# A hybrid attention and linear-attention layer on one core: the opening with tokens, parameters and modulation blocks laid out by the host

## The chip, the core and the metric

The kernel runs on one core of one Trainium2 chip. The core has five engines that run side by side, each with its own queue of instructions: TensorE (matrix products), VectorE, ScalarE, GpSimd and SyncE. In the profile they are PE (with PEld for its weight loads), DVE, ACT, POOL and SP. Data come from the chip's memory through 16 DMA engines; SP issues nearly all of the transfers, from a queue that keeps its order. The metric is the device time of one execution in microseconds (us). Lower is better.

## The reference: what is computed

One layer over 256 latent tokens `x` and 256 context tokens `ctx`, each of 2048 channels, all in float32. The parts that matter here are the modulated norm at its start and the input projection that follows:

```python
mod_x = split(silu(c)     @ w_mod + b_mod, 6)     # shift, scale, gate, shift, scale, gate
mod_c = split(silu(c_ctx) @ w_mod + b_mod, 6)
h_x = rms_norm(x,   g_mix) * (1 + mod_x[1]) + mod_x[0]
h_c = rms_norm(ctx, g_mix) * (1 + mod_c[1]) + mod_c[0]
proj = h @ w_in          # columns for attention, linear attention, merge gates
```

`rms_norm` divides each token by the root of the mean of its 2048 squares. After the projection come windowed attention with the context as further keys, gated linear attention that starts from the context's end states, a gated merge, an output projection, and a convolutional feed-forward block with its own modulated norm. The output is the latent stream, 256 x 2048.

## The kernel before, in words

**Products.** The 2048 input channels are 16 tiles of 128 partitions (`KT`). Every product in float32 precision is made of three faster ones: an operand is split into a high and a low part, and high x high, high x low and low x high are summed. Weights come in tiles of 128 x 2 x 512 values (`wload`, line 209; 512 KB), and `wsplit_raw` (line 223) makes the high part on ScalarE (line 227) and the low part on VectorE (line 228). `proj_T` (line 277) gives the result with channels on the partitions, in steps of 256 columns; `proj_nat` (line 238) gives it with tokens on the partitions, in steps of 512 columns.

**Modulation.** `mod_both` (line 329) computes shift or scale of `x` and `ctx` for some channel tiles. It loads blocks of `w_mod` of 1 MB each (`mraw`, line 340) and multiplies them with SiLU(c), held in `cS`, by small products that use a quarter of the array each (line 344). The result goes through a transpose on VectorE (line 347), a selecting product `pcol` (line 354), four copies and the addition of the bias (lines 357 and 360).

**The opening (lines 114 to 160 and 549 to 619).** The tokens arrive with tokens on the partitions. The sum of squares of a token block is one instruction, on ScalarE for one block and on VectorE for the other (lines 456 and 457). 32 transposes for `x` and 32 for `ctx` on TensorE (line 465) bring the channels onto the partitions, and copies (lines 471 and 473) take them out of PSUM into `xr`. `factors` makes the norm's factors per token, and `factor_row` (line 483) spreads them as a row by a product of ones with a diagonal matrix. Parameters come as rows through GpSimd's queue and are turned by TensorE (`columns`, line 138). `idle` (line 543) gives TensorE transposes without use, `warm` in the profile.

**Groups.** The input channels are taken in five groups, of 2, 2, 4, 4 and 4 tiles (`groups`, line 433). For each group the modulated, split tokens (`h00hi`, `h00lo` for x, `h10hi`, `h10lo` for ctx) are made by `affine_scale` and `affine_shift`, and then go through four blocks of 512 columns of `w_in`: two with x alone (QB), one with x and ctx (KB, `kbt`), one with x and ctx (VB, `vb0`). The modulation of the next group is computed meanwhile: `bg_steps` holds its steps, and `tick` (line 192) puts some of them between the products, `bg_rate` steps for each weight tile. `mid` is a function called in the middle of a weight tile's products. What has to wait for a result on another engine is put off by `defer`.

**What sets the order.** `load` (line 102) chains the loads of the opening in the order of the program on SP's queue; each waits there until its buffer is free. `pe_seq` (line 74) pins TensorE's instructions to the program's order while `opening` holds something; this ends with the second group. `in_order` fixes the order of single pairs. Buffers of 8 KB per partition come from one pool of 16 (`M`): the tokens, the partial results `kbt` and `vb0` and the split tokens keep some, and the `mraw` blocks use what is left. Weight tiles (`raw`) have seven buffers, their split parts three pairs.

After the groups follow the gates' low-rank product (`wlr`, `plr`, line 679) and the rest of the layer. `mod_latent` (line 365) computes the other modulation parts on VectorE beside later products, with SiLU(c) as a row `csrow`, loaded (line 379) from a copy `csd` in the chip's memory, which line 132 writes. That load's place on SP's queue is left to the planner that orders the instructions.

Of the kernel before, what the change touches and what calls it, by code (L numbers as in the profile page):

```python
# [16 lines left out]
P = 128  # L17
# [9 lines left out]
DFF = 5632  # L27
SCALE = HD ** -0.5


def layer_kernel(ctx, tc, A, out):
# [15 lines left out]
    w_mod = A["w_mod"][0]  # L47
# [49 lines left out]
    def turn_b(*a):  # L97
        return pe_seq(after(PE.transpose(*a)))  # L98

    chain = [None]  # L100

    def load(dst, src):

        d = nc.sync.dma_start(dst, src).ins
        if chain and chain[-1] is None:
# [8 lines left out]
    ident = cst.tile([P, P], F32, name="ident")  # L114
    load(ident, A["k_ident"])
    x00 = M("x00", [P, D])
    load(x00, A["x"][0][0:P, :])
    crow = sm.tile([32, P], F32, name="crow", tag="t128", bufs=2)
    nc.scalar.dma_start(crow[0:16, :], A["c"][0].rearrange("(k p) -> k p", p=P))
    nc.scalar.dma_start(crow[16:32, :], A["c_ctx"].rearrange("(k p) -> k p", p=P))  # L120
    sel = cst.tile([P, 34], F32, name="sel")
    G.dma_start(sel, A["k_sel"])
    ones = cst.tile([P, P], F32, name="ones")
    V.memset(ones, 1.0)

    silu_c = S.activation(crow, crow, AF.Silu)
    with tc.issue_after(silu_c.ins):
        S.preload_act_table_set("natural_log_exp_and_others")
    cS = W2("fb", "cS", [P, KT, 32])
    V.memset(cS, 0.0)  # L130
    csd = dram.tile([KT, P], F32, name="csd")
    G.dma_start(csd, crow[0:16, :])
    pt = bank("pc0", (P, 32))
    PE.transpose(pt, crow, ident[:32, :32])
    for i in range(2):
        V.tensor_copy(cS[:, :, i], pt[:, 16 * i:16 * i + 16])

    def columns(name, parts, eng=G, put=None):
        rows = sm.tile([P, P], F32, name="rows", tag="t128", bufs=2)
        n = 0  # L140
        for ap in parts:
            k = ap.shape[0] // P
            eng.dma_start(rows[n:n + k, :], ap.rearrange("(k p) -> k p", p=P))
            n += k
        t = cst.tile([P, n], F32, name=name)

        def turn():
            pt = bank("pt_" + name, (P, P))
            turn_b(pt[:, :n], rows[:n, :], ident[:n, :n])
            V.tensor_copy(t, pt[:, :n])  # L150

        if put is None:
            turn()
        else:
            put(turn)
        return t

    turn_c1 = []
    c1 = columns("c1", [A["b_mod"][0], A["g_mix"][0], A["g_ffn"][0]], put=turn_c1.append)
    bmod, gmix, gffn = c1[:, 0:96], c1[:, 96:112], c1[:, 112:128]  # L160

# [167 lines left out]
    def mod_both(part, t0, n, dst, put=None):  # L329


        a = []
        c0, w = part * D + t0 * P, n * P
        nk = 16 // n

        def step(k0):
# [3 lines left out]
            load(raw, w_mod[k0 * P:(k0 + nk) * P, c0:c0 + w].rearrange("(c p) d -> p c d", p=P))  # L340
# [24 lines left out]
    def mod_latent(parts, begin=None):  # L365
# [67 lines left out]
    groups = [(0, 2), (2, 2), (4, 4), (8, 4), (12, 4)]  # L433
# [3 lines left out]
    xr = [M(f"xr{i}", [P, 8, T]) for i in range(4)]  # L437
# [4 lines left out]
    def load_tokens(s):  # L442
        x = []
        for t in range(2):
            x_ = x00
            if s or t:
                x_ = M(f"x{s}{t}", [P, D])
                load(x_, A["ctx" if s else "x"][0][t * P:(t + 1) * P, :])
            x.append(x_)
        return x  # L450

    def square(eng, x_, t, ss):

        junk = (kbt, vb0)[t].rearrange("p a b -> p (a b)")
        if eng is S:
            return S.activation(junk, x_, AF.Square, accum_out=ss[:, t:t + 1]).ins
        return V.scalar_tensor_tensor(junk, x_, 1.0, x_, op0=ALU.mult, op1=ALU.mult,
                                      accum_out=ss[:, t:t + 1]).ins

    def turn_tokens(s, t, x_):  # L460
        for g in range(4):
            pt = bank("ptx", (P, 4, P), side=True)
            for k in range(4):
                kt = g * 4 + k
                i = PE.transpose(pt[:, k, :], x_[:, kt * P:(kt + 1) * P], ident)
                if not s + t + kt:
                    opening[:] = [i.ins]
                pe_seq(i)
            dst = xr[2 * s + g // 2][:, (g % 2) * 4:(g % 2) * 4 + 4, t * P:(t + 1) * P]
            if g % 2:  # L470
                i = V.tensor_copy(dst, pt).ins
            else:
                S.activation(dst, pt, AF.Copy)
        return i

    def factors(ss):
        cols = rms_scale(ss, D, [P, 2])
        dgs = [sm.tile([P, P], F32, name="dg", tag="t128", bufs=2) for _ in range(2)]
        for t in range(2):
            V.tensor_scalar(dgs[t], ident, cols[:, t:t + 1], None, op0=ALU.mult)  # L480
        return dgs

    def factor_row(s, dgs):

        pr = bank("pr", (P, T), side=True)
        for t in range(2):
            pe_seq(PE.matmul(pr[:, t * P:(t + 1) * P], ones[:, 0:P], dgs[t], start=True, stop=True))
        r = W2("fa", f"rrow{s}", [P, T])
        S.activation(r, pr, AF.Copy)
        rrow1.append(r)  # L490
# [19 lines left out]
    def affine_scale(s, t0, n):  # L510
        sc = scale1[:, s, t0:t0 + n]
        V.scalar_tensor_tensor(sc, sc, 1.0, gmix[:, t0:t0 + n], op0=ALU.add, op1=ALU.mult)
# [34 lines left out]


    x_t = load_tokens(0)
    sums = [sm.tile([P, 2], F32, name="ss0", tag="ss0", bufs=2) for _ in range(2)]  # L550
    square(S, x_t[0], 0, sums[0])
    i = turn_tokens(0, 0, x_t[0])
    in_order(i, square(V, x_t[1], 1, sums[0]))
    turn_tokens(0, 1, x_t[1])
    turn_c1[0]()
# [17 lines left out]
    early.extend(wload(w_in[0:2 * P, QB + j * 512:QB + j * 512 + 512]) for j in range(2))  # L573
    x_t = load_tokens(1)
    raws = [wload(w_in[0:2 * P, c:c + 512]) for c in (KB, VB)]
# [4 lines left out]
    sq0 = square(S, x_t[0], 0, sums[1])  # L580
    sq1 = square(V, x_t[1], 1, sums[1])
    proj_T(w_in, QB + 512, kts, [h_all(0)], add_to(lambda i: qb0[2 + i], True))
    in_order(last_lo[0], sq1)
    hold_hi.append(sq0)
    hold.append(sq1)
    early.append(wsplit_raw(raws[0]))
    dgs = factors(sums[1])
    for t in range(2):
        turn_tokens(1, t, x_t[t])
    early.append(wsplit_raw(raws[1]))  # L590
    (a0, a1, ea), (b0, b1, eb) = mods[1]
    a0()
    factor_row(1, dgs)
    a1()
    affine_scale(1, *groups[0])
    affine_shift(1, *groups[0])

    def mid_k():
        ea()
        b0()  # L600
        for s in range(2):
            affine_scale(s, *groups[1])

    def mid_v():
        eb()
        hi.append(affine_shift(0, *groups[1])[1])

    def evac_v(i, b):
        if i < 2:
            V.tensor_copy(vb0[:, i, :], b)  # L610
        else:
            in_order(hi[0], S.activation(vb0[:, i, :], b, AF.Copy).ins)

    hi = []
    proj_T(w_in, KB, kts, [h_all(0), h_all(1)], add_to(lambda i: kbt[:, i, :], True), mid=mid_k)
    b1()
    early.extend(wload(w_in[2 * P:4 * P, c:c + 512]) for c in (QB, QB + 512, KB, VB))
    proj_nat(w_in, 0, VB, kts, h_xc, evac_v, mid=mid_v)
    affine_shift(1, *groups[1])

    for gi, (t0, n) in enumerate(groups):
# [6 lines left out]
        flush()  # L628
        if gi + 1 < len(groups):
            bg_steps.extend(mods[gi + 1][0] + mods[gi + 1][1])  # L630
            ticks = 4 * ((n + 1) // 2)
            bg_rate[:] = [(1.4 if gi > 1 else 1.0) * len(bg_steps) / ticks + 0.01, 0.0]
        if t0 == 8:
            more_h(1)
        for s in range(2):
# [3 lines left out]
            if s == 0:  # L639
                for j in range(2):  # L640
                    proj_T(w_in, QB + j * 512, kts, [h_all(0)], add_to(lambda i, j=j: qb0[2 * j + i], False))
        proj_T(w_in, KB, kts, [h_all(0), h_all(1)], add_to(lambda i: kbt[:, i, :], False))
        proj_nat(w_in, 0, VB, kts, h_xc, add_to(lambda i: vb0[:, i, :], False), mid=flush if gi == 1 else None)
        opening.clear()

    chain.clear()


    cw0 = columns("cw0", [A["conv_w"][0, 0], A["b_gate_f"][0], A["b_gate_b"][0]])
    nbg = cw0[:, 88:104]  # L650
    V.tensor_scalar(nbg, nbg, -1.0, None, op0=ALU.mult)
# [20 lines left out]
    G.dma_start(wlr, w_in[:, LR:LR + 32].rearrange("(k p) d -> p k d", p=P))  # L672
    pl = bank("plr")
# [383 lines left out]
    cw1 = columns("cw1", [A["conv_w"][0, 1]], put=lambda fn: defer(6, fn))  # L1057
    cw2 = columns("cw2", [A["conv_w"][0, 2]], put=lambda fn: defer(6, fn))
    more = []
# [231 lines left out]
```

## Time and profile before

| | us |
|---|---|
| median of 3 runs | 2002.11 |
| lowest and highest | 2001.83, 2002.72 |
| the profiled execution | 2002.13 |
| its span in the trace | 2000.3 |
| TensorE busy in the span | 1972.3 |
| first product of the projection | 31.41 after the span's start |
| first product of the second group (2 tiles) | 63.35 |
| first product of the third group (4 tiles) | 88.39 |
| first `plr` product | 212.67 |

The profile is of one execution. A row of its timeline has the start in us after the span's start, the length in us, the engine, the line of the kernel, the operation, what is written and read, and how many such instructions are merged into the row; in brackets stand the time that the engine was idle before and what ended it. The engine SPq is SP's queue, where a row is the issue of a transfer. The granted clock is TensorE's, 1.00 being full.

### The profile page before, as it was taken

The numbers are of one execution on the slowest core, as the hardware profiler recorded it, in microseconds if no ns is written. First come the engines' busy times: TensorE is split into PE (matmuls) and PEld (weight loads), VectorE is DVE, ScalarE is ACT, GpSimd is POOL, SyncE is SP. The second block draws the span as 40 slices with busy tenths as digits, with TensorE's granted clock in tenths as the row PEclk, the third lists the DMA queues.
The fourth block names the chain that finished last, engine by engine and source line by source line (L and its number), as shares of the span: only waits on it lengthen the run. The fifth ranks groups of instructions, "written<-read, shape, count | busy, mean of one in ns | idle before, by whom it ended". The sixth has DMA issues, their size and how long they took to land.

```text
span 2000.3 us, 27285 instructions
## 1 busy us (share of the span) xinstructions
PE 1972.3 (99%) x10418; PEld 1645.9 (82%) x10418; DVE 1385.3 (69%) x2128; ACT 961.1 (48%) x1395; POOL 46.9 (2%) x67
## 2 busy tenths in 40 slices
PE   7999999999999999999999999999999999999999
PEld 5779888888877777888888888888888888888887
DVE  4666567867858877877766455888887555667754
ACT  4323454653345656444444444655555334555532
POOL 1001010111000000000000000000000000000000
PEclk8999999999999999999999999999999999999999
DMA  9986222226753356788888665587876556555563
GB/s 324 385 294 206 70 72 92 89 94 198 234 173 117 119 168 218 262 289 290 294 283 284 232 206 193 167 293 255 269 255 229 194 192 191 188 189 189 190 214 112
DMA packets 198371, 415.64 MB, mean 208 GB/s; under 512 B 12500, under 2 KB 20980, under 8 KB 197216
## 3 DMA queue, kind: packets, MB, share of 16 engines
q1 hardware_dynamic: 196656, 409.06, 61.3%
q0 software_dynamic: 1520, 4.83, 0.8%
q8 instruction: 81, 1.33, 0.3%
q14 instruction: 50, 0.41, 0.1%
q10 hardware_dynamic: 64, 0.02, 0.0%
HBM read 411.73 MB, written 2.12 MB: 207 GB/s over the span
## 4 chain that ended last, share of the span: by engine, by line
PE 59%; DVE 0%; ACT 0%; issue 0%; DVEq 0%
PE acc L83 47%; PE accs L83 12%; PE pto L98 0%; PE ptx L98 0%; DVE yd L1231 0%; DVE yd L1225 0%; ACT yo L1112 0%; ACT whi L227 0%; ACT x1T L1120 0%; DVE dg L1153 0%; ACT h L506 0%; DVE h L507 0%; DVE x1T L505 0%; PE pr L1155 0%; DVE fac L1150 0%
## 5 line engine op out<-in xcount | busy, mean ns | idle before, releaser
L228 DVE TENSOR_TENSOR wlo<-raw,whi 128x1024 fp32r<-128x1024 f32 x568 | 694.5, 1224 | 448.2 <-ACT whi L227 406.9
L227 ACT ACTIVATE whi<-raw 128x1024 fp32r<-128x1024 f32 x568 | 602.2, 1061 | 816.1 <-PE acc L83 644.6
L83 PE MATMUL acc<-h,whi 128*128 128x512 f32 x704 | 176.6, 392 | 0.6 <-DVE h L507 0.6
L83 PE MATMUL accs<-h,whi 128*128 128x512 f32 x704 | 176.3, 392 | 0.0
L83 PEld LDWEIGHTS acc<-h,whi 128*128 128x128 f32 x704 | 126.5, 189 | 23.6 <-DVE h L507 0.9
L83 PEld LDWEIGHTS accs<-h,whi 128*128 128x128 f32 x704 | 126.6, 189 | 22.6
L83 PE MATMUL acc<-whi,h00hi 128*128 128x512 f32 x352 | 139.9, 397 | 1.2 <-DVE v3l L62 0.7
L83 PE MATMUL acc<-whi,h01hi 128*128 128x512 f32 x352 | 139.2, 395 | 0.0
L83 PE MATMUL acc<-whi,h00lo 128*128 128x512 f32 x352 | 138.2, 393 | 0.0
L83 PE MATMUL acc<-whi,h01lo 128*128 128x512 f32 x352 | 137.8, 392 | 0.0
L83 PE MATMUL acc<-whi,ah 128*128 128x512 f32 x352 | 137.0, 389 | 0.0
L83 PE MATMUL acc<-whi,al 128*128 128x512 f32 x352 | 137.0, 389 | 0.0
L83 PEld LDWEIGHTS acc<-h,wlo 128*128 128x128 f32 x704 | 96.2, 190 | 7.0
L83 PEld LDWEIGHTS accs<-h,wlo 128*128 128x128 f32 x704 | 96.1, 190 | 6.8
L83 PE MATMUL acc<-wlo,h00hi 128*128 128x512 f32 x352 | 98.4, 394 | 0.0
L83 PE MATMUL acc<-h,wlo 128*128 128x256 f32 x704 | 98.3, 282 | 0.0
L83 PE MATMUL accs<-h,wlo 128*128 128x256 f32 x704 | 98.2, 282 | 0.0
L83 PE MATMUL acc<-wlo,h01hi 128*128 128x512 f32 x352 | 97.8, 394 | 0.0
L83 PE MATMUL acc<-wlo,ah 128*128 128x512 f32 x352 | 94.4, 389 | 0.0
L387 DVE CUSTOM_DVE_ANT_0 raw<-raw,csrow,c 128x1024 f32<-128x1024 f32 x64 | 81.2, 1284 | 0.0
L83 PEld LDWEIGHTS acc<-whi,h00hi 128*128 128x128 f32 x352 | 66.4, 189 | 16.5 <-DVE v3l L62 1.1
L83 PEld LDWEIGHTS acc<-whi,ah 128*128 128x128 f32 x352 | 66.1, 188 | 13.7
(388 smaller groups left out, 3525.7 us busy)
## 6 DMA issues: line engine op xcount, KB each, us to landing
raw<-in_w_in SPq DMA_DIRECT2D x208, 512.0 KB, 4.4
raw<-in_w_up SPq DMA_DIRECT2D x176, 512.0 KB, 3.6
raw<-in_w_modT SPq DMA_DIRECT2D x128, 512.0 KB, 4.5
raw<-in_w_down SPq DMA_DIRECT2D x88, 512.0 KB, 3.6
mraw<-in_w_mod SPq DMA_DIRECT2D x32, 1024.0 KB, 12.9
raw<-in_w_attn_o SPq DMA_DIRECT2D x32, 512.0 KB, 5.0
raw<-in_w_gla_o SPq DMA_DIRECT2D x32, 512.0 KB, 5.1
raw<-in_w_out SPq DMA_DIRECT2D x32, 512.0 KB, 3.6
```

Of the source, the lines that this page charges most:

```text
L83: r = pe_seq(PE.matmul(*a, **k))
L227: j = S.activation(hi[:, 0:n, :], raw[:, 0:n, :], AF.Copy).ins
L228: i = V.tensor_tensor(lo[:, 0:n, :], raw[:, 0:n, :], hi[:, 0:n, :].bitcast(F32), op=ALU.subtract).ins
L387: i0 = V.tensor_tensor_reduce(out=raws[i], in0=raws[i], in1=row[0], scale=1.0, scalar=d if h else bmod[:, b0:b0 + 1], op0=ALU.mult, op1=AL ...
```

## The change

The host lays out four things anew before the launch; the kernel's arithmetic on them is the same.

- `x` and `ctx` come with the channels on the partitions (`xT`, `ctxT`), each in four loads of 512 KB, straight into `xr`. The transposes on TensorE and their copies go.
- The blocks of `w_mod` for shift and scale come so that each partition of a 1 MB block is one run of 8 KB (`w_mod01`).
- The identity, the biases, the norm weights, the selecting matrix and c, c_ctx as columns come as one array `k_pack` on ScalarE's queue. `conv_w`, `conv_b` and the gates' biases come as one array `k_cols` on GpSimd's queue, behind an instruction `gate` that reads the scale of the last group; the other loads of that place stand behind it too. The transposes in `columns` go.
- The sums of squares: ScalarE squares pieces of 128 x 1024, VectorE folds some of them by additions, and TensorE multiplies what is left with a matrix of ones, which sums over the partitions and spreads the sum. For x these are twelve products of 256 columns, for ctx one.
- The factor row is now computed on 128 x 256 values (logarithm, exponential, one Newton step); its factor of -0.5 moves into `gm1`.
- The first group is computed for x alone through all four blocks, then KB and VB for ctx with the split weights kept. Idle transposes stand at new places.
- While the second group's products run, the eight modulation steps of the third are placed by a list: 1, 2, 1 and 1 in the middle of and between its products, the other three behind its last product.
- TensorE's order stays pinned until the end of the fourth group, and `csrow`'s load is placed behind the load that precedes it in the program.

The diff, cut to its core:

```diff
-    load(ident, A["k_ident"])
-    x00 = M("x00", [P, D])
-    load(x00, A["x"][0][0:P, :])
...
+    pack = cst.tile([P, 322], F32, name="pack")
+    nc.scalar.dma_start(pack, A["k_pack"])
...
+    load_tokens(0)
...
+    S.activation(cS[:, :, 0:2], pack[:, 290:322].rearrange("p (k s) -> p k s", s=2), AF.Silu)
...
-            load(raw, w_mod[k0 * P:(k0 + nk) * P, c0:c0 + w].rearrange("(c p) d -> p c d", p=P))
+            load(raw, A["w_mod01"][part, t0 + k0 // nk].rearrange("p (c d) -> p c d", c=nk))
...
-            load(row[0], csd[8 * h:8 * h + 8, :].rearrange("k p -> (k p)").partition_broadcast(P))
+            before = last_load[0]
+            in_order(before, load(row[0], csd[8 * h:8 * h + 8, :].rearrange("k p -> (k p)").partition_broadcast(P)))
...
+    def square_sums(s):
+
+        pr = bank("pr", (P, T), side=True)
+        sums = [[], [], [], []]
+        whole = None
+        for i in range(4):
+            x_ = xr[2 * s + i // 2][:, (i % 2) * 4:(i % 2) * 4 + 4, :]
+            q = wr.tile([P, 4, T], F32, name="sq", tag="raw")
+            S.activation(q, x_, AF.Square)
+            if s == 0 and i in (0, 3):
+                sums[i] = [q[:, k, :] for k in range(4)]
+                continue
+            h = q[:, 0:2, :]
+            V.tensor_tensor(h, h, q[:, 2:4, :], op=ALU.add)
+            if s and whole is not None:
+                V.tensor_tensor(whole, whole, h, op=ALU.add)
+            elif s:
+                whole = h
             else:
-                S.activation(dst, pt, AF.Copy)
...
+                sums[i] = [h[:, k, :] for k in range(2)]
+        if s:
+            V.tensor_tensor(whole[:, 0, :], whole[:, 0, :], whole[:, 1, :], op=ALU.add)
+            sums[3] = [whole[:, 0, :]]
+        parts = sum(sums, [])
+
+        def add_up(lo, hi):
+            for i in range(lo, hi):
+                pe_seq(PE.matmul(pr, ones[:, 0:P], parts[i], start=(i == 0), stop=(i == len(parts) - 1)))
...
+    def factor_row(pr):
...
+        V.tensor_scalar(v, pr, 1.0 / D, EPS, op0=ALU.mult, op1=ALU.add)
+        S.activation(r, v, AF.Ln)
+        S.activation(r, r, AF.Exp, scale=-0.5)
+        V.tensor_tensor(t, r, r, op=ALU.mult)
+        V.tensor_tensor(t, t, v, op=ALU.mult)
+        V.scalar_tensor_tensor(r, t, -3.0, r, op0=ALU.add, op1=ALU.mult)
...
+    idle(20)
+    pr, add_up = square_sums(0)
+    add_up(0, 4)
+    idle(6)
+    add_up(4, 8)
+    V.tensor_scalar(gm1, gmix, -0.5, None, op0=ALU.mult)
     (a0, a1, ea), (b0, b1, eb) = mods[0]
+    add_up(8, 12)
+    factor_row(pr)
     a0()
-    dgs = factors(sums[0])
+    idle(6)
     a1()
-    factor_row(0, dgs)
-    idle(8)
+    raws = [wload(w_in[0:2 * P, QB:QB + 512])]
+    idle(6)
     ea()
+    idle(6)
     b0()
     affine_scale(0, *groups[0])
-    idle(12)
+    idle(14)
     b1()
+    raws.extend(wload(w_in[0:2 * P, c:c + 512]) for c in (QB + 512, KB, VB))
     idle(6)
     eb()
     idle(14)
...
+    proj_T(w_in, KB, kts, [h_all(0)], lambda i, b: S.activation(half(i, 0), pair_of(b), AF.Copy))
+    wv = wsplit_raw(raws[3])
+    early.append(wv)
+    pr, add_up = square_sums(1)
+    proj_nat(w_in, 0, VB, kts, h_x, lambda i, b: S.activation(vb0[:, i, :], b, AF.Copy))
     (a0, a1, ea), (b0, b1, eb) = mods[1]
+    add_up(0, 1)
+    factor_row(pr)
     a0()
...
     affine_scale(1, *groups[0])
     affine_shift(1, *groups[0])
...
+    idle(6)
+    a1()
+    idle(6)
+    ea()
+    early.extend([wk, wv])
+    proj_T(w_in, KB, kts, [h_all(1)], lambda i, b: S.activation(half(i, T), pair_of(b), AF.Copy), mid=b0)
+    for s in range(2):
+        affine_scale(s, *groups[1])
+    proj_nat(w_in, 0, VB, kts, [h_tok(1, 0), h_tok(1, 1)],
+             lambda i, b: S.activation(vb0[:, 2 + i, :], b, AF.Copy), mid=b1)
     early.extend(wload(w_in[2 * P:4 * P, c:c + 512]) for c in (QB, QB + 512, KB, VB))
...
+    eb()
+    idle(8)
+    affine_shift(0, *groups[1])
     affine_shift(1, *groups[1])
...
+            bg_rate[:] = [1.4 * len(bg_steps) / ticks + 0.01, 0.0]
+            if gi == 1:
+                bg_rate[:] = [0.0, 0.0]
+                steps = iter([1, 2, 1, 1, 2])
...
-        opening.clear()
+        if gi > 2:
+            opening.clear()
...
+    gate = cst.tile([P, 2], F32, name="gate")
+    gate_op = G.tensor_tensor(gate, scale1[:, 0, 12:14], scale1[:, 0, 12:14], op=ALU.add)
+    behind_gate = tc.issue_after(gate_op.ins)
...
+    G.dma_start(cw, A["k_cols"])
```

More of the change, by code (lines that the diff above doesn't have):

```diff
@@ L128, in layer_kernel @@
         S.preload_act_table_set("natural_log_exp_and_others")
-    cS = W2("fb", "cS", [P, KT, 32])
-    V.memset(cS, 0.0)
     csd = dram.tile([KT, P], F32, name="csd")
[L132 to L160, printed above, removed]
+    G.dma_start(csd, crow)
+    gm1 = cst.tile([P, KT], F32, name="gm1")
     bg_steps = []
@@ L332, in mod_both @@
         a = []
-        c0, w = part * D + t0 * P, n * P
+        w = n * P
         nk = 16 // n
@@ L440, in layer_kernel @@
     vb0 = M("vb0", [P, 4, 512])
[L442 to L471, printed above, removed]
-            else:
-                S.activation(dst, pt, AF.Copy)
-        return i
@@ L476, in factors @@
[L476 to L489, printed above, removed]
+    def square_sums(s):
+        pr = bank("pr", (P, T), side=True)
+        sums = [[], [], [], []]
+        whole = None
+        for i in range(4):
+            x_ = xr[2 * s + i // 2][:, (i % 2) * 4:(i % 2) * 4 + 4, :]
[10 more added lines that the diff above has]
+                whole = h
+            else:
+                sums[i] = [h[:, k, :] for k in range(2)]
[6 more added lines that the diff above has]
+                pe_seq(PE.matmul(pr, ones[:, 0:P], parts[i], start=(i == 0), stop=(i == len(parts) - 1)))
+        return pr, add_up
```

132 lines of the change are left out of this document (65 added, 67 removed).

## The prediction

> **What bounds the kernel now.** I read the page first (totals and the chain that ended last), then the table of windows, then the queue's own waits, then the timeline of the first 90 us. First the page:
>
> ```profile
> span 2000.3 us, 27285 instructions
> PE 1972.3 (99%) x10418; PEld 1645.9 (82%) x10418; DVE 1385.3 (69%) x2128; ACT 961.1 (48%) x1395; POOL 46.9 (2%) x67
> PE 59%; DVE 0%; ACT 0%; issue 0%; DVEq 0%
> ```
>
> TensorE is busy nearly everywhere, and the traced chain consists of its work. So the change can win in three ways only: dense products begin earlier, TensorE is given less that is not a product, or a hole closes. The table of windows (us; TensorE, weight loads, VectorE, ScalarE, GpSimd; granted clock; DMA share; GB/s) shows the hole:
>
> ```profile
> 0.00:10.00 10.00, 3.41 (x15) 3.02 (x16) 1.61 (x5) 5.02 (x6) 3.47 (x10) 1.00 0.61 228
> 10.00:20.00 10.00, 5.10 (x37) 3.51 (x35) 5.51 (x13) 2.44 (x6) 0.00 (x0) 0.76 0.90 282
> 60.00:70.00 10.00, 10.00 (x77) 6.43 (x76) 7.48 (x14) 4.19 (x8) 0.00 (x0) 1.00 1.05 387
> 8.00:9.00 1.00, 1.00 (x6) 1.00 (x5) 0.16 (x1) 1.00 (x1) 0.00 (x0) 1.00 0.47 173
> ```
>
> In the first 20 us the DMA moves 228 and 282 GB/s where later it moves 387. The queue's waits and the timeline of the first 32 us name the reason:
>
> ```profile
> SPq L104 <- DMA csd<-crow: 7.8, 1, 7.8
> ```
>
> ```profile
> 1.19 0.90 SPq L104 DMA_DIRECT2D x<-in_x  x2
> 4.94 1.28 ACT L126 ACT_TABLE_LOAD   x1 [4.94 <-DMA crow<-in_c_ctx]
> 6.56 1.28 ACT L128 ACT_TABLE_LOAD   x1
> 6.83 6.22 PE L465 MATMUL ptx<-ident,x 128*128 128x128 f32 x32
> 7.85 1.91 ACT L456 ACTIVATE kb<-x 128x2048 f32<-128x2048 f32 x1
> 9.88 0.33 SPq L104 DMA_DIRECT2D csrow<-csd  x1
> 10.26 7.25 SPq L104 DMA_DIRECT2D mraw<-in_w_mod  x4
> 17.70 1.93 PE L95 MATMUL pm<-mraw,cS 128*32 128x256 f32 x16 [4.54 <-DMA mraw<-in_w_mod]
> 23.50 1.91 PE L546 MATMUL warm<-ident 128*128 128x128 f32 x8
> 27.89 1.07 PE L95 MATMUL pm<-mraw,cS 128*32 128x256 f32 x16
> 28.89 0.87 PE L546 MATMUL warm<-ident 128*128 128x128 f32 x6
> 29.03 0.45 DVE L347 STREAM_TRANSPOSE mtr<-pm 128x256 f32<-128x256 f32 x1 [1.32 <-PE pm L95]
> 29.69 0.23 PE L95 MATMUL pcol<-mtr,sel 128*32 128x16 f32 x2
> 29.86 1.75 PE L546 MATMUL warm<-ident 128*128 128x128 f32 x14
> 29.96 0.65 DVE L357 COPY shift<-pcol 32x4 f32<-32x4 f32 x4 [0.49 <-PE pcol L95]
> 30.85 0.91 ACT L522 ACTIVATE h00hi<-xr,shift 128x256 fp32r<-128x256 f32 x2 [1.83 <-DVE shift L360]
> 31.41 0.38 PE L83 MATMUL acc<-h00hi,whi 128*128 128x256 f32 x1
> ```
>
> The row `csrow<-csd`, wanted hundreds of us later, stands on SP's queue ahead of the first modulation blocks and waits 7.8 us for a small write. The blocks leave at 10.26, TensorE waits for them at 17.70, and the first product is at 31.41.
>
> **Part by part. 1: the opening.** The csrow load is now placed behind the last load before it, so SP issues x and then the blocks. By the shapes, bytes up to the block b1 are: parameters 0.17 MB, x 2.10, four blocks 4.19, one weight tile 0.52, together 6.98 MB. x's 2.1 MB ended at about 8.45 (the 8 to 9 us window, 0.47 busy); at 387 GB/s they began at 2.9. So b1 lands at 2.9 + 18.0 = 20.9. By the nearest rows the rate may be 282, which gives 27.7.
>
> TensorE's own order gives a later bound. ScalarE starts on the first parameters at 4.94 as now (bounds: 2.9, where the stream starts, and 8.45, where x was in; 4.94 is the nearest row); two table loads and two short SiLUs (0.3 each, the gap up to the second table load) end at 8.1; four squares of 128x1024 at half of 1.91 end at 11.9. VectorE's two adds lie beside them. TensorE does 20 transposes at the slow clock (1.91/8 = 0.24 each) from 4.94 to 9.7, then twelve products with ones. Their price is not shown by such a product; the nearest are the four-quadrant products of the same width:
>
> ```profile
> 212.67 0.64 PE L679 MATMUL plr<-h00hi,wlr 128*32 128x256 f32 x8
> 213.12 0.40 PE L679 MATMUL plr<-h00lo,wlr 128*32 128x256 f32 x4
> ```
>
> Eight instructions, two per product, in 0.45: four quadrants run beside each other, so one float32 product of 256 columns takes 0.44 at the full clock, 0.88 at half. I take 0.44. Twelve cost 5.3, six transposes 0.75 (1.75/14 = 0.125 each): the ones end at 15.7, after the last square. Then a0 1.07, idle 0.75, a1 1.07, idle 0.75, the scale's end 0.2, idle 0.75, b0 1.07, idle 1.75: b1 starts at 23.15, with its data there since 20.9. From b1 to the first product the trace has 31.41 - 27.89 = 3.5, and this piece stays. **First product at 26.7, that is -4.7 us.** The row factors (a chain of some 2.8) end at 18.5, before the scales at 20.4: hidden.
>
> **2: transposes of ctx.** They lie on TensorE's path:
>
> ```profile
> 37.83 1.47 PE L465 MATMUL ptx<-ident,x 128*128 128x128 f32 x12
> 43.85 1.07 PE L95 MATMUL pm<-mraw,cS 128*32 128x256 f32 x16 [0.25 <-ACT xr L473]
> 44.85 0.71 PE L487 MATMUL pr<-dg,ones 128*128 128x128 f32 x4
> ```
>
> They go: **-6.0**; the factor products, 0.6 of path, become one of 0.44: **-0.15**. Their evacuations (8 PSUM copies over the two streams) leave ScalarE and VectorE; squares and adds come in their stead.
>
> **3: x first, then context.** The number of products is the same. These pairs give their step:
>
> ```profile
> 32.67 0.28 PE L83 MATMUL acc<-h00lo,whi 128*128 128x256 f32 x1
> 32.79 0.28 PE L83 MATMUL acc<-h00hi,whi 128*128 128x256 f32 x1
> 56.93 0.39 PE L83 MATMUL acc<-whi,h00hi 128*128 128x512 f32 x1
> 57.16 0.39 PE L83 MATMUL acc<-whi,h00lo 128*128 128x512 f32 x1
> ```
>
> 0.12 and 0.227. Products on x alone: 72 x 0.12 + 12 x 0.227 = 11.4, plus 0.5 for the first low part as now, so they end at 38.6. ctx's last piece (10.66 MB) lands at 30.4; its squares and VectorE's folding (eight passes, of at most 0.7) are done by 34 to 36. Hidden, with 3 to 5 us of cover. Then pr 0.44, a0, idle, a1, idle, the scale's end: 43.0. Added idle here and before group 1: 20 transposes, **+2.5**.
>
> The factor chain of ctx is new on the path: VectorE, ScalarE twice, VectorE three times, each 0.4, then the two rows below, about 4.1 after pr, against 4.0 of fill.
>
> ```profile
> 46.02 0.88 DVE L515 SCALAR_TENSOR_TENSOR xr<-xr,scale,rrow 128x256 f32<-128x256 f32 x2 [1.10 <-ACT rrow L489]
> L347 DVE STREAM_TRANSPOSE mtr<-pm 128x512 f32<-128x512 f32 (+1 forms) x10 | 6.1, 609 | 13.6 <-PE pm L95 13.6
> ```
>
> I take a wait of 0.4. After group 0's context, eight idle transposes stand against a chain of 1.5: another 0.6. Group 1 now has five modulation steps between its products and three behind them, at about 1.05 each, as here:
>
> ```profile
> 87.40 1.06 PE L95 MATMUL pm<-mraw,cS 128*32 128x512 f32 x8
> 88.39 0.39 PE L83 MATMUL acc<-h00hi,whi 128*128 128x256 f32 x1
> ```
>
> The last three have group 2's shift behind them: transpose 0.75 ((6.1 - 4 x 0.45)/6), selection 0.35, copies and add 0.9, the high part 0.5, some 2.6, in which only the next group's first step (1.0) works. TensorE's queue is in order: everything of group 2 waits behind it. Waits after: 0.5 + 0.4 + 0.6 + 2.6 = 4.1. Before: from 31.41 to 88.39 there are 57.0 us, of which products 33.9 (two groups of 96 x 0.12 + 24 x 0.227), thirteen steps 13.1, selections 1.2, transposes 6.0 and factors 0.6 make 54.8, so 2.2 of waits. Difference 1.9, less the 0.9 of the step that now lies inside one: **+1.0**.
>
> So group 2 starts at 88.39 - 4.7 - 6.0 - 0.15 + 2.5 + 1.0 = 81.0. Its weights come behind 26.9 MB, at 2.9 + 69.5 = 72.4: the queue has 8 us of cover.
>
> **4: the rest.** Groups 2 to 4 keep their work. Four column transposes leave later stages (chain of the end, start and length):
>
> ```profile
> 852.81 0.14 PE pt_cw L98
> ```
>
> at most 0.14 in each of four places: **-0.5**. The one packed load in their place waits on GpSimd for the last group's scale; behind it stand the mask, the gate weights and wlr. That scale is made during group 3, and group 4's own products (33.9 by the steps above) lie between it and the first use: I cost it at nothing. Without that cover wlr's load would stand open ahead of the `plr` products.
>
> **Sum:** -4.7 - 6.0 - 0.15 + 2.5 + 1.0 - 0.5 = -7.85. The profiled execution took 2002.13 us (span 2000.3 and 1.8 around it), 0.02 above the median: **1994.3 us.**
>
> **Rivals.**
>
> *A, less waiting.* If parameters land at 2.9, the opening follows b1's landing: first product 24.4, 2.3 earlier; and if the list order fills the boundary of group 2, 2.6 more goes. Together 1989.4. For it: the DMA is then dense from the start. Against: TensorE's order is pinned.
>
> *B, ctx's factor late.* Should its squares stand on ScalarE behind the evacuations of the products on x (ready at 38.6), four squares, the last adds and the sum add some 4.5: 1998.8. Against: in the trace the Square of ctx waited for its load alone:
>
> ```profile
> 33.20 1.92 ACT L456 ACTIVATE kb<-x 128x2048 f32<-128x2048 f32 x1 [0.49 <-DMA x<-in_ctx]
> ```
>
> *C, slow clock in the opening, so that the change brings nothing there.* The clock column has 0.76 from 10 to 20 us. Were it half until about 26: twenty transposes to 9.7, twelve ones at 0.88 with six transposes among them (1.4) to 21.7, a0 at 1.93 and six transposes to 25.1; from there at the full clock a1, idle, the scale's end, idle, b0 and idle 5.6 to 30.7, then 3.5: first product at 34.2 instead of 26.7, 2001.8, no change. For it: 17.70 shows 1.93 for what takes 1.07 at 27.89. Against: there TensorE had been without work since 13.1; here it is fed from 4.94 on. [...]
>
> *D, the other side: the DMA becomes the bound.* The loads are one strict chain, and group 2's first weights stand behind all modulation blocks of group 2. From 353 GB/s downward they come too late (26.9 MB by 79); below some 307 the kernel is slower by 0.2%. At the 282 of the second window they land at 98.3, group 2 starts at 100.6: +12.2 - 0.5, 2013.8. For it: 282 was measured with these blocks. Against: that window holds the start-up, and the new blocks have longer runs (8 KB a partition) than those that ran at 387. [...]
>
> **Chances.** Forecast 0.62 (own range 1991 to 1997.5), A 0.14, B 0.10, C 0.08, D 0.06. 0.2%, about what a measurement of this kernel can tell from no change, is 4.0 us. Faster: forecast, A and half of B, 0.81; same: half of B, C: 0.13; slower: D, 0.06. Range 1988.5 to 2000.5: it takes in A and B with about 1 us beyond each, and leaves out C and D.
>
> **What would show it.** SP's queue without a wait for csd, blocks issued by 3 to 4 us; first product at 26.7 (25 to 28.5); no gap over 1 us before the products on ctx; group 2 at 81 (78 to 84.5), and the first `plr` product, now at 212.67, some 7 us earlier; DMA near 387 GB/s from 5 to 70 us. Wrong it would be by a first product after 30, by ScalarE's squares of ctx after the evacuations, or by weight splits of group 2 that wait for their load.

## The result, and the profile after

The changed kernel takes 2006.62 us (median of 15 runs, 2004.87 to 2007.83), the kernel before 2002.2 us beside it (15 runs, 2001.6 to 2002.8). The ratio is 1.0021, with a 95% interval of 1.0013 to 1.0029: slower by 0.2%, where 1994.3 was forecast. The profiled execution took 2007.47 us; its span is 2004.8.

The page's totals after the change:

```profile
span 2004.8 us, 27258 instructions
...
PE 1975.5 (99%) x10425; PEld 1650.6 (82%) x10425; DVE 1380.9 (69%) x2112; ACT 960.7 (48%) x1392; POOL 42.4 (2%) x59
```

They look like those of before. The stages do not. The table of windows after (TensorE, weight loads, VectorE, ScalarE, GpSimd; granted clock; DMA share; GB/s), and behind it the row of before for 90 to 100 us:

```profile
0.00:10.00 10.00, 4.59 (x22) 4.60 (x23) 0.82 (x3) 4.53 (x6) 1.39 (x6) 1.00 0.80 250
10.00:20.00 10.00, 10.00 (x74) 7.53 (x74) 3.52 (x7) 4.15 (x6) 0.00 (x0) 1.00 1.02 424
60.00:70.00 10.00, 10.00 (x73) 9.03 (x73) 3.79 (x5) 1.06 (x1) 0.00 (x0) 0.87 0.33 124
90.00:100.00 10.00, 8.31 (x49) 7.35 (x49) 4.75 (x9) 5.78 (x9) 0.00 (x0) 0.66 1.02 415
```

```profile
90.00:100.00 10.00, 10.00 (x83) 7.46 (x82) 6.33 (x11) 3.35 (x6) 0.00 (x0) 1.00 1.05 387
```

The opening is repaired: from 10 to 20 us the DMA moves 424 GB/s where it moved 282, and TensorE is busy throughout, with a clock column of 1.00 where it was 0.76. Two later rows are worse than before: the clock is 0.87 from 60 to 70 us, and 0.66 from 90 to 100, where it was 1.00. A busy share of 10.00 beside a clock of 0.87 is not ten microseconds' worth of products at the full clock: up to 61.3 they step by 0.21 to 0.22 here instead of 0.12.

The timeline of the opening after the change:

```profile
2.74 1.01 SPq L104 DMA_DIRECT2D mraw<-in_w_mod  x2
...
9.94 2.64 PE L448 MATMUL pr<-sq,ones 128*128 128x256 f32 x8
...
13.07 3.62 PE L448 MATMUL pr<-sq,ones 128*128 128x256 f32 x16
...
27.41 0.38 PE L83 MATMUL acc<-h00hi,whi 128*128 128x256 f32 x1
...
39.71 0.60 PE L448 MATMUL pr<-sq,ones 128*128 128x256 f32 x2
...
45.44 0.24 PE L95 MATMUL pcol<-mtr,pack 128*32 128x16 f32 x2 [1.51 <-DVE mtr L326]
```

The blocks leave at 2.74 instead of 10.26, eight products with ones (two instructions each) take 3.62 (the four before them 2.64, at a slower step), the first product comes at 27.41 instead of 31.41, and the sum for ctx follows the products on x at 39.71 without a wait. The last row is the first loss: the selection of the second group's scale, which stands on TensorE ahead of the products on ctx, waits 1.51 us for its transpose, which is in VectorE's queue behind the factor and the tokens of ctx.

Then the second group. This is TensorE's timeline, with the waits in brackets; behind it stand the rows of ScalarE and VectorE for the same stretch:

```profile
55.94 0.38 PE L83 MATMUL acc<-h00hi,whi 128*128 128x256 f32 x1 [0.85 <-ACT h00hi L495]
...
57.20 0.38 PE L83 MATMUL acc<-h00lo,whi 128*128 128x256 f32 x1 [0.88 <-DVE h00lo L496]
...
58.73 0.39 PE L83 MATMUL acc<-h00lo,whi 128*128 128x256 f32 x1 [1.03 <-DVE h00lo L496]
...
59.58 0.42 PE L83 MATMUL acc<-h00hi,whi 128*128 128x256 f32 x1
59.80 0.42 PE L83 MATMUL acc<-h00lo,whi 128*128 128x256 f32 x1
```

```profile
54.44 1.06 ACT L207 ACTIVATE whi<-raw 128x1024 fp32r<-128x1024 f32 x1
55.38 0.51 ACT L495 ACTIVATE h00hi<-xr,shift 128x256 fp32r<-128x256 f32 x1
55.78 1.05 ACT L207 ACTIVATE whi<-raw 128x1024 fp32r<-128x1024 f32 x1
```

```profile
55.53 1.23 DVE L208 TENSOR_TENSOR wlo<-raw,whi 128x1024 fp32r<-128x1024 f32 x1 [0.39 <-ACT whi L207]
56.67 0.48 DVE L496 SCALAR_TENSOR_TENSOR h00lo<-xr,shift,h00hi 128x256 fp32r<-128x256 f32 x1
57.06 1.22 DVE L208 TENSOR_TENSOR wlo<-raw,whi 128x1024 fp32r<-128x1024 f32 x1
58.20 0.48 DVE L496 SCALAR_TENSOR_TENSOR h00lo<-xr,shift,h00hi 128x256 fp32r<-128x256 f32 x1
```

Read each queue downward. TensorE wants `h00hi`, then `h00lo`, for the first channel tile and for the second. ScalarE does a weight split (1.06) ahead of each `h00hi`, and VectorE a weight split (1.2) ahead of each `h00lo`, though these weights are wanted many products later. TensorE has three holes between 55.1 and 58.7, 2.8 of 3.6 us. Right behind them, at 59.58, the step from one product to the next is 0.22 instead of 0.12: the clock has fallen to half, and it stays there until 62.85 (granted: 0.53 from 59.58 to 62.85, 1.00 from there to 70).

The start of the third group, in the same order (ScalarE, then TensorE):

```profile
88.58 1.71 ACT L495 ACTIVATE h00hi<-xr,shift 128x256 fp32r<-128x256 f32 x4 [25.95 <-DVE shift L339]
...
90.59 1.04 ACT L207 ACTIVATE whi<-raw 128x1024 fp32r<-128x1024 f32 x1
...
91.69 0.58 PE L83 MATMUL acc<-h00hi,whi 128*128 128x256 f32 x1 [3.18 <-ACT whi L207]
...
92.28 0.41 PE L83 MATMUL acc<-h00hi,whi 128*128 128x256 f32 x1
...
92.49 0.41 PE L83 MATMUL acc<-h00lo,whi 128*128 128x256 f32 x1
```

ScalarE was idle for 25.95 us. The first `whi` of the third group, 1.04 us of work that needs no shift, stood behind five token activations (four `h00hi`, one `h10hi`) that did need it. So TensorE, which needs both, waited 3.18 us, and after that ran its first 24 products in 5.3 us (91.69 to 96.99, at a granted clock of 0.52) instead of 24 x 0.12 = 2.9.

**Where the gain went.** The second group started 7.4 us earlier than before (55.94 against 63.35). It lasted 35.75 us against 25.04, of which some 2 are more modulation products (72 instructions start in it against 56, eight in 1.05), and the third group's slow start took another 2.4. So 7.4 were won and 13.1 lost: the fifth group ends some 5.5 us later than before (at 215.1 against 209.6), and the span is 4.5 longer. The first `plr` product, after, is the row

```profile
215.17 0.64 PE L666 MATMUL plr<-h00hi,wlr 128*32 128x256 f32 x8
```

only 2.5 us behind the 212.67 of before, because before it stood behind 24 products of the next weight tile (3.0 us) that now follow it. They began there with

```profile
209.62 0.36 PE L83 MATMUL acc<-h00hi,whi 128*128 128x256 f32 x1
```

A marker that moves past other work misleads; the last product of the group doesn't.

### The profile page after: what moved, and what is told of

The parts are those of the page before. It is cut to its first block, busy times and chain, and to the rows that moved or that the text cites. A ratio compares the mean times of both kernels' runs of the same rounds, so it can differ in the third digit from the quotient of the medians.

```text
span 2004.8 us, 27258 instructions
## 1 busy us (share of the span) xinstructions
PE 1975.5 (99%) x10425; PEld 1650.6 (82%) x10425; DVE 1380.9 (69%) x2112; ACT 960.7 (48%) x1392; POOL 42.4 (2%) x59
## 4 chain that ended last, share of the span: by engine, by line
PE 59%; DVE 0%; ACT 0%; issue 0%; DVEq 0%
PE acc L83 46%; PE accs L83 12%; PE pto L98 0%; PE ptx L98 0%; DVE yd L1213 0%; DVE yd L1207 0%; ACT yo L1095 0%; ACT whi L207 0%; ACT x1T L1103 0%; DVE dg L1136 0%; ACT h L479 0%; DVE h L480 0%; DVE x1T L478 0%; PE pr L1138 0%; DVE fac L1133 0%
## 5 line engine op out<-in xcount | busy, mean ns | idle before, releaser
L367 DVE CUSTOM_DVE_ANT_0 raw<-raw,csrow,pack 128x1024 f32<-128x1024 f32 x64 | 81.1, 1282 | 0.0
L83 PEld LDWEIGHTS acc<-whi,al 128*128 128x128 f32 x352 | 66.1, 188 | 13.7
```

The costliest lines, as they stand in the source:

```text
L83: r = pe_seq(PE.matmul(*a, **k))
L367: i0 = V.tensor_tensor_reduce(out=raws[i], in0=raws[i], in1=row[0], scale=1.0, scalar=d if h else bmod[:, b0:b0 + 1], op0=ALU.mult, op1=AL ...
```

## The experiments

Theory O (order): the new loss comes from the places of weight splits in ScalarE's and VectorE's queues at the starts of the second and third group, and from the clock that falls behind the holes. Rival L (load): TensorE's steps come so late in the second group that the block buffers run out; SP waits for them (81.7 us in 16 times over the first 260 us, against 31.2 before), the DMA falls to 124 GB/s from 60 to 70 us, and weights arrive late.

```profile
SPq L104 <- PE pm L95: 81.7, 16, 25.9
```

A second question was what each useful part is worth alone. All medians are beside runs of the kernel before on the same chip (its medians there: 2002.1 to 2002.4). A difference between two runs is one of medians; the intervals of the ratios reach some 2 us to either side, so that a difference of 2 us or less rests on the rows as much as on the times. The diffs show the core of each edit.

### The load of csrow alone

In the kernel before:

```diff
+        last_load[:] = [d]
...
-            load(row[0], csd[8 * h:8 * h + 8, :].rearrange("k p -> (k p)").partition_broadcast(P))
+            before = last_load[0]
+            in_order(before, load(row[0], csd[8 * h:8 * h + 8, :].rearrange("k p -> (k p)").partition_broadcast(P)))
```

> The kernel before with one edit: the csrow load stands behind the load that precedes it in the program. If SP's queue is what held the opening back, the modulation blocks are issued by 3 us instead of 10.3, the first product comes at 24 to 26 instead of 31.4, and since nothing else moves, 5 to 7 us of the time go: about 1996. If the opening is bound by TensorE's own transposes and the slow clock instead, the first product stays above 29 and the gain is under 2 us.

Measured: 1998.06 us, ratio 0.9979 (0.9969 to 0.9988), -4.3 us, a little less than the 5 to 7 expected.

```profile
26.23 0.38 PE L83 MATMUL acc<-h00hi,whi 128*128 128x256 f32 x1
```

The first product comes at 26.23 (24 to 26 was expected), a little before that of the whole change. The one moved load is worth the whole opening as far as its first product goes. Of the 5.2 us won here 3.9 are left at the third group's start (84.47). TensorE waits for modulation blocks 4.4 us in 7 times, 3.5 of it ahead of the first product and 0.9 behind it, and from 60 to 70 us the DMA moves 387 GB/s without a gap: the loads have become what the opening waits for.

```profile
PE pm L95 <- DMA mraw<-in_w_mod: 4.4, 7, 1.8
...
60.00:70.00 10.00, 9.46 (x77) 5.70 (x77) 6.20 (x16) 1.06 (x1) 0.00 (x0) 1.00 1.05 387
```

### Weight splits behind the tokens of x, second group

In the changed kernel, the second and third weight split are held behind the high and low tokens of x:

```diff
-    affine_shift(0, *groups[1])
+    i, j = affine_shift(0, *groups[1])
+    hold.extend([None, i, i])
+    hold_hi.extend([None, j, j])
     affine_shift(1, *groups[1])
```

> The kernel after with one edit: the second and third weight splits of the second group stand behind the split of x on ScalarE and VectorE. Order theory (the second group starts late because weight splits stand ahead of x's low parts in VectorE's queue, and the waits let TensorE's clock fall): the first 24 products of the group take some 3 us instead of 6.9, the clock stays full there, 3 to 4 us go. Load theory (the groups wait for blocks and weights that leave SP late, since the block buffers run out): no change beyond 1 us.

Measured: 2002.73 us, ratio 1.0002 (0.9992 to 1.0011), 3.9 less than the changed kernel. Three rows of TensorE's timeline:

```profile
26.32 0.38 PE L83 MATMUL acc<-h00hi,whi 128*128 128x256 f32 x1
...
54.69 0.39 PE L83 MATMUL acc<-h00hi,whi 128*128 128x256 f32 x1 [0.65 <-ACT h00hi L495]
...
87.08 0.45 PE L83 MATMUL acc<-h00hi,whi 128*128 128x256 f32 x1 [3.18 <-ACT whi L207]
```

The opening, which the edit does not touch, was 1.1 us faster in this execution (first product at 26.32 against 27.41; in all six kernels here that share this opening 26.3 to 26.9). That is nearly all of the 1.25 us by which the second group starts earlier. In the second group the two holes ahead of `h00lo` are gone, the clock is 1.00 from 60 to 70 us, and the third group starts 4.6 us earlier, 3.5 without the opening, still with its own hole of 3.18. The DMA still moves only 165 GB/s there:

```profile
60.00:70.00 10.00, 10.00 (x83) 7.46 (x81) 3.94 (x7) 0.00 (x0) 0.00 (x0) 1.00 0.50 165
```

So these holes came from the order, and not from the loads.

### The third group's first weight split ahead of its tokens as well

The edit above stays in, and to it comes:

```diff
+        if gi == 2:
+            early.append(wsplit_raw(wload(w_in[t0 * P:(t0 + 2) * P, QB:QB + 512])))
         for s in range(2):
```

> The kernel after with two edits: that of e2_lows, and the first weight tile of the third group is loaded and split ahead of that group's modulated tokens. Order theory: ScalarE has the weight's high part ready before the tokens, the 3.2 us wait at the third group's start goes, and so does the slow clock behind it (2 us): together with e2_lows 7 to 9 us less than after, about 1998 to 2000, below before. Load theory: the split would wait for its load in the new place, the group starts no earlier, and the time is that of e2_lows.

Measured: 1999.04 us, ratio 0.9983 (0.9974 to 0.9993), 3.7 less again. ScalarE's row, then TensorE's:

```profile
73.78 1.06 ACT L207 ACTIVATE whi<-raw 128x1024 fp32r<-128x1024 f32 x1 [14.55 <-DVE scale L485]
...
84.79 0.39 PE L83 MATMUL acc<-h00hi,whi 128*128 128x256 f32 x1 [0.64 <-ACT h00hi L495]
```

The same split now begins at 73.78, and the hole is 0.64. In the changed kernel the weight tile was issued by SP at 73.23, 17 us before its split began at 90.59:

```profile
73.23 0.38 SPq L104 DMA_DIRECT2D raw<-in_w_in  x1
```

In the kernel of this run the DMA moves only 156 GB/s from 60 to 70 us, and still the hole is closed. Rival L is out for it.

### Useless work in the third group's hole

In the changed kernel, 24 transposes without use on TensorE ahead of the third group; the order of ScalarE and VectorE stays:

```diff
+        if gi == 2:
+            pd_ = bank("pf", (P, P), side=True)
+            for _ in range(24):
+                pe_seq(PE.transpose(pd_, ident, ident))
```

> The kernel after with 24 transposes without use on TensorE in the hole ahead of the third group (3 us of added work); the order on ScalarE and VectorE is the same. If the clock falls because TensorE stands idle there, the hole stays but the group's first 24 products run at 0.12 us a step again: 1.5 to 2.5 us less than after in spite of the added work. If the clock has another cause, or the products are slow because they wait for operands, the time is the same or up to 3 us longer.

Measured: 2004.33 us, ratio 1.0009 (0.9999 to 1.0018), 2.3 less than the changed kernel.

```profile
86.74 2.84 PE L613 MATMUL pf<-pack 128*128 128x128 f32 x24
...
90.86 0.39 PE L83 MATMUL acc<-h00hi,whi 128*128 128x256 f32 x1 [0.28 <-ACT whi L207]
...
91.42 0.28 PE L83 MATMUL acc<-h00hi,whi 128*128 128x256 f32 x1
91.54 0.28 PE L83 MATMUL acc<-h00lo,whi 128*128 128x256 f32 x1
```

The group still starts when ScalarE's split allows it (0.83 us earlier than in the changed kernel, as its opening was 0.8 faster), but its products now step by 0.12. So the fall of the clock is a cost of its own beside the wait: 5.3 - 2.9 = 2.4 by the rows, 2.3 by the times.

### The list of the second group's steps undone

In the changed kernel, the third group's modulation steps are spread evenly, two to a weight tile:

```diff
             if gi == 1:
-                bg_rate[:] = [0.0, 0.0]
+                bg_rate[:] = [len(bg_steps) / ticks + 0.01, 0.0]
+            if False:
                 steps = iter([1, 2, 1, 1, 2])
```

> The kernel after with the list of steps undone: two modulation steps of the third group at each weight tile of the second, none behind its last product. The planner then puts the weight split of the third group ahead of its tokens on ScalarE by itself. Order theory: the 3.2 us wait at the third group's start and the slow clock behind it go, and the three steps with their chain (2.6 us) too: 5 to 7 us less than after, some 2000 to 2001.5. Rival, that the steps had to stand late because their blocks land late: TensorE waits for blocks inside the second group, and the time stays within 2 us of after.

Measured: 1998.1 us, ratio 0.9979 (0.997 to 0.9989), 8.5 less than the changed kernel, more than the 5 to 7 expected.

```profile
54.19 1.92 PE L95 MATMUL pm<-mraw,cS 128*32 128x512 f32 x16
...
57.90 0.39 PE L83 MATMUL acc<-h00lo,whi 128*128 128x256 f32 x1 [1.03 <-DVE h00lo L496]
...
83.49 0.39 PE L83 MATMUL acc<-h00hi,whi 128*128 128x256 f32 x1 [1.49 <-ACT h00hi L495]
```

Without the list the planner puts the third group's splits ahead of its tokens by itself. Two steps now stand on TensorE ahead of the second group (54.19) and cover two of its three holes; one of 1.03 is left, and the clock is 1.00 from 50 to 70 us, which the expectation had not counted. What is left is a hole of 1.49 us in front of the group: its shift is still selected behind the last product, and ScalarE waits for it. A hole of 0.61 follows, and the clock is 0.83 from 80 to 90 us.

### Both repairs

The held splits and the list undone, in one kernel:

```diff
+    hold.extend([None, i, i])
+    hold_hi.extend([None, j, j])
...
+                bg_rate[:] = [len(bg_steps) / ticks + 0.01, 0.0]
```

> e2_lows and e5_nolist together: both holes closed by order and the steps spread. If the holes add up, 9 to 11 us less than after, some 1996 to 1998. If the blocks' landing sets the pace of the second group once its waits are gone, no better than 1999.

Measured: 1996.71 us, ratio 0.9971 (0.996 to 0.9982).

```profile
81.87 0.39 PE L83 MATMUL acc<-h00hi,whi 128*128 128x256 f32 x1 [1.50 <-ACT h00hi L495]
...
80.00:90.00 10.00, 7.90 (x49) 6.26 (x46) 6.72 (x16) 5.31 (x10) 0.00 (x0) 0.83 1.02 412
```

The third group starts 9.8 us earlier than in the changed kernel (1.0 of it is the opening of this execution), with the hole of 1.50 and the fall of the clock left.

### The load of csrow and the layout of the blocks, in the kernel before

The edit of csrow's load from the first run, and:

```diff
-            load(raw, w_mod[k0 * P:(k0 + nk) * P, c0:c0 + w].rearrange("(c p) d -> p c d", p=P))
+            load(raw, A["w_mod01"][part, t0 + k0 // nk].rearrange("p (c d) -> p c d", c=nk))
```

> e1_csrow with the modulation blocks laid as in the change (one run of 8 KB per partition). In e1_csrow TensorE waits seven times for blocks, some 4 us in all, at 387 GB/s. If the DMA's rate is what those waits hang on, the rate rises to some 415 GB/s as in the kernel after, the waits shrink, and 1.5 to 4 us more go: 1994 to 1996.5. If the rate comes from the other loads, the time is that of e1_csrow, 1998.

Measured: 1995.57 us, ratio 0.9967 (0.9954 to 0.9979), 2.5 less than with csrow alone.

```profile
24.82 0.38 PE L83 MATMUL acc<-h00hi,whi 128*128 128x256 f32 x1
...
81.49 0.50 PE L83 MATMUL acc<-h00hi,whi 128*128 128x256 f32 x2
...
60.00:70.00 10.00, 10.00 (x86) 7.08 (x79) 8.00 (x21) 0.07 (x1) 0.00 (x0) 1.00 1.01 415
...
PE pm L95 <- DMA mraw<-in_w_mod: 1.5, 2, 1.3
```

The rate rises from 387 to 415 GB/s, and the waits for blocks fall from 4.4 to 1.5 us. Two edits of a few lines, with the old tokens, transposes and order, bring 6.6 us of the 7.85 forecast for all. The first product comes at 24.82, 1.5 us or more ahead of every kernel here with the new opening.

### The third group's shift selected earlier

In the kernel with both repairs, the shift of the third group is selected in the middle of the last weight tile, as in the kernel before:

```diff
-        proj_nat(w_in, 0, VB, kts, h_xc, add_to(lambda i: vb0[:, i, :], False), mid=mid)
+        proj_nat(w_in, 0, VB, kts, h_xc, add_to(lambda i: vb0[:, i, :], False), mid=flush if gi == 1 else None)
```

> e6_lowsteps with one edit: what was put off (the selection and bias of the third group's shift) is carried out in the middle of the second group's last weight tile, as in the kernel before, not behind its last product. In e6_lowsteps TensorE waits 1.5 + 0.6 us for the tokens at the third group's start, the clock mean falls to 0.83 in 80 to 90 us, and the selection stands on the path. Order theory: all three go, 3 to 4 us less than e6_lowsteps, some 1993. If the wait is replaced by one for VectorE, which then evacuates four banks and makes the tokens at once, 1 to 2 us less.

Measured: 1994.25 us (1993.68 to 1994.61), ratio 0.996 (0.9946 to 0.9974). It is the fastest of all; 2.5 us less than with both repairs, between the 3 to 4 and the 1 to 2 that were expected under the two readings.

```profile
80.11 1.06 PE L95 MATMUL pm<-mraw,cS 128*32 128x512 f32 x8
...
81.10 0.38 PE L83 MATMUL acc<-h00hi,whi 128*128 128x256 f32 x1
...
80.00:90.00 10.00, 9.61 (x77) 6.67 (x80) 7.16 (x15) 5.93 (x11) 0.00 (x0) 1.00 1.02 409
```

No hole is left in front of the third group, which starts at 81.10, and the clock is 1.00. Against csrow and blocks alone the rest of the change, so repaired, is worth 1995.57 - 1994.25 = 1.3 us, a difference that the overlapping intervals of the two ratios do not make certain.

## Why the prediction was wrong

**Step 1 was right.** First product -4.0 us against -4.7 forecast. A product with ones takes 3.62/8 = 0.45 once the clock is full (0.44 taken). The parameters landed 0.5 later than taken (5.43 against 4.94), and TensorE's chain starts with them. The first four products with ones took 0.62 each (9.94 to 12.42) where 0.44 was taken: their instructions step by 0.43 up to 11.22 and by 0.22 from 11.55 on. So the slow steps, beside which the clock column has 1.00, ended between these two; that they would end at 9.7 was my estimate, and no run shows it. These two make more than the 0.7; the 20 idle transposes before were somewhat faster than taken (4.27/20 = 0.21 each for 0.24).

```profile
5.43 1.28 ACT L134 ACT_TABLE_LOAD   x1 [5.43 <-DMA pack<-in_k_pack]
```

**Step 2 was right** as far as it can be seen: no transpose of ctx is left on the path, and its sum follows the products on x at once. No run measures its 6.0 us alone.

**Step 3 failed, in its term "Waits after: 0.5 + 0.4 + 0.6 + 2.6 = 4.1", +1.0 against before.** I followed TensorE's queue, which keeps its order (the products on ctx, whose `h10hi` ScalarE had made by 44.51, began at 45.60, behind the selection that waited 1.51 us), and took every operand as ready when its inputs are. But ScalarE and VectorE worked in an order too (the `whi` of 90.59 behind the wait of 25.95, the `h00lo` of 56.67 behind a `wlo` of 1.23), and I asked of no operand what stood ahead of it there. The signs were there: I wrote that the third group's weights would be loaded at 72.4, 8 us ahead of need, and did not ask where their split stands between those tokens. The trace of before could not show the new order, but the danger should have had a price: a split of 1.06 or 1.22 ahead of a token's 0.5. Nor did any term hold the clock's fall, though the table of before has a 0.76. The error by stages, up to the end of the fifth group:

| stretch | forecast us | measured us | difference |
|---|---|---|---|
| start to first product | 26.7 | 27.41 | +0.7 |
| to the second group | 26.4 | 28.53 | +2.1 |
| second group | 28.1 | 35.75 | +7.65 |
| clock at half in the third group | 0 | 2.4 | +2.4 |

Together 12.85; 0.5 of it is won back later (step 4), and the median lies 2006.62 - 1994.3 = 12.3 above the forecast. In the second line 1.1 is the wait ahead of the products on ctx (1.51 for 0.4): factor and tokens of ctx took 4.7 us behind the sum where 4.1 was taken, with 3.6 of work on TensorE beside them where 4.0 was taken, and the transpose of 0.44 stood behind them. Another 0.25 is the first hole (0.85 for 0.6). In the third, TensorE is idle for 6.77 us of its 35.75 (0.88 + 1.03 + 3.18, and two of 0.84 in which a selection waits for the transpose of the step just ahead of it) where the forecast had 1.6 (its 2.6 less the step of 1.0 that works in it). That is 5.2; 1.5 of the remaining 2.5 is the half clock from 59.2 to 62.85, in which 18 products take 3.7 us instead of 2.2. Some 1.7 us in these two lines are small gaps between products that I have not traced. Two slips in my sums change nothing here: (6.1 - 4 x 0.45)/6 is 0.72 and not 0.75, and 2.1 MB that end at 8.45 began at 3.0 and not 2.9.

So the failed term, forecast at 3.1 us of idle time (4.1 less the step of 1.0), measured 0.34 + 1.51 + 0.85 + 6.77 = 9.5, and 1.5 + 2.4 = 3.9 us of half clock stood in no term.

The trace after shows both, the order and the clock. On ScalarE a split of 1.04 us stood behind a wait of 25.95. On TensorE the hole of 3.18 us was followed by half clock for 5.3 us, and so were the three of 0.85, 0.88 and 1.03 with a few products between them, for 3.7 us.

**Step 4** held within what can be told: from the end of the fifth group the span wins back 1.0 against 0.5 forecast (5.5 late there, 4.5 at the end).

**The rivals.** A (less waiting) came out the other way. B did not occur: the sum of ctx was ready. Nor did C: the slow steps ended between 11.2 and 11.6 us and not at 26. D, the only one on the slower side, had the right sign for the wrong reason: the DMA moved 400 to 424 GB/s in each 10 us from 10 to 60, and the 124 of 60 to 70 us is a consequence, since SP waits there for a buffer that TensorE's late steps hold (12.7 us in one wait). The kernel with the splits held and the split of the third group ahead ran 7.6 us faster while the loads stayed as sparse (286 GB/s from 50 to 70 us, 270 in the changed kernel). Of the signs that I had named, the early blocks (2.74) and the first product inside 25 to 28.5 came; the gap above 1 us ahead of ctx's products (1.51) and the third group at 91.69 spoke against. Weight splits that wait for their load, named as a sign of being wrong, did not come: the split that held TensorE up waited in its queue.

**A number that agrees by luck.** With the three order repairs the kernel takes 1994.25 us and its third group starts at 81.10, against 1994.3 and 81.0 in the forecast. This does not bear the sum out, for it is not the kernel of the forecast: with the list undone the 2.6 us behind the last product leave the waits (4.1 becomes 1.5, and +1.0 becomes -0.7), so that the same sum would give 1992.6 and 79.3. The kernel lies some 1.7 us above that. TensorE still waits 1.52 us ahead of the products on ctx where 0.4 was taken, which is 1.1 of it.

**What stays open.** The changed kernel's runs spread over 3.0 us, those of the kernel before over 1.2 and those of the last experiment over 0.9. That the clock falls and comes back at different times from run to run would explain it, but was not shown. Measured is this: in the kernel with the useless work, whose holes there are 0.86, 0.88 and 1.03, the products step by 0.21 from 0.38 us behind the third hole (58.35 against 57.97), in the changed kernel from 0.64 behind it (59.37 against 58.73). And with one and the same opening the first product came at 26.3 to 27.4. Removing the longer pinning of TensorE's order was not run; the last experiment keeps it and is 12.4 us faster than the changed kernel, so it is not where most of the loss lay. The change without csrow's new place was not run either.

## What to carry to other kernels

When a change moves work that feeds a group of products, write down for each operand of the first products what stands ahead of it in its own engine's queue, not only in TensorE's: in these traces an instruction that waited held up what stood behind it, and a weight split of 1 us in the wrong place made a hole of 3.18 us where 0.64 was left with the order mended, and cost 2.4 us of clock behind it. Measure the small parts of a large change alone: here one load's place and one layout gave 6.6 us, and all the rest lost 11 until its order was mended.

## What the hardware showed that was not expected

- **Longer runs moved faster.** With the modulation blocks in runs of 2 KB a partition the DMA moved 387 GB/s from 60 to 70 us, and 415 with nothing changed but runs of 8 KB.
- **Useless work made the kernel faster:** 24 transposes, 2.84 us of TensorE's time, took 2.3 us off.
- **Short holes halved the clock** where they were close: idle 2.8 of 3.6 us was enough, with no hole above 1.03, and 18 products took 3.7 us instead of 2.2. One short hole alone did not do it here: behind the 1.51 us ahead of 45.44 in the same trace, and behind the 1.03 in the kernel without the list, the products step by 0.12 from the second on.
